# A three-product compression and VectorE sample projections in a one-core NSA / mLSTM step

## The chip, the cores and the metric

The kernel is one launch on one core of a Trainium2 chip. The metric is device time in microseconds (us). A profiled execution gives, beside its time, the start and duration of every instruction on TensorE (PE, with its weight loads PEld), VectorE (DVE), ScalarE (ACT), GpSimd (POOL) and SyncE (SP, which issues most DMAs).

## The reference, cut to what matters

Two layers run for a prompt of 512 tokens and for 8 samples with one new token each, 520 columns in all; the model width is 1024. Layer 0 is native sparse attention, layer 1 an mLSTM, and each adds its output to x. Two places matter here. In layer 0, rows of k and v are compressed: blocks of 32 rows that start every 16 rows, for 1024 cached rows per sample and for the prompt's 512.

```python
seg = rows.reshape(B, n_seg, CMP_STRIDE, 2, N_KV_HEADS, HEAD_DIM)   # segments of 16 rows
w1r = w1f.reshape(2, CMP_R, CMP_STRIDE, HEAD_DIM, CMP_HID)          # CMP_R = 2
part = jnp.einsum('bnrchd,cjrde->bnjche', seg, w1r)
for j in range(CMP_R):
    hid = hid + part[:, j:j + n_cmp, j]
summ = jnp.einsum('bnche,ced->bnchd', jax.nn.silu(hid), w2)
```

So, with A and B the two halves of w1, block i is A s(i) + B s(i+1) over the segments s, then a SiLU and a small second product. In layer 1, q, k and v come from block-diagonal weights, 4x4 blocks over 2048 inner columns:

```python
q = jnp.einsum('btnj,nji->btni', cb, w_qkv[0])   # cb: c = silu(conv) in blocks of 4
k = jnp.einsum('btnj,nji->btni', cb, w_qkv[1])
v = jnp.einsum('btnj,nji->btni', xb, w_qkv[2])   # xb: xm in blocks of 4
```

All results are fp32. The kernel gets that precision from PE either with plain fp32 operands or by splitting each operand into a high and a low part in the fp32r format and summing three fp32r products (`mm3`, L601: hi x hi, hi x lo, lo x hi).

## The kernel before, in words

The program has seven stages, and in each the order of instructions was laid down ahead of time. In four of them a recorder `Rec` (L426) notes every engine call as a piece, where successive PE calls into one PSUM bank form one piece, and then emits the pieces in the order of a written list of numbers (L465). In the other three a `Plan` (L324) holds coarser operations with named dependences, and a list orders those (L352). Each engine works through its own instructions strictly in the order of emission. A second list per stage (MOVED...) names pieces that run on another engine than the code says (`swapped`, L481): an ACT copy goes to DVE, a DVE copy to ACT, and subtractions, multiplications and additions change between DVE and POOL. Counted in order of execution the lists are: 0 CALLS0 (L1028: norm, k/v projections, compression, gates), 1 CALLS2 (L1419), 2 ORDER0 (L1629: attention), 3 CALLS1 (L1956: output projection of layer 0, then the mLSTM's input projection, convolution, SiLU, values, gates), 4 ORDER1 (L2312: z projections, first eight steps over the samples' state matrices), 5 ORDER2 (L2709: the mLSTM cell, the other 24 state steps, most of the output projection) and 6 CALLS3 (L2760: the rest, final norm).

List 0. `kv_tile(i)` (L866) projects one of twelve 128-column tiles of k and v: two chunks of 260 tokens, 24 fp32r products each, scaled out of PSUM into `kvt` on DVE. `cmp_unit(b, c)` (L786) compresses one sample b for k (c = 0) or v (c = 1). It loads eight pages (`praw`), splits them in pieces of 1024 columns into `phi` (ACT) and `plo` (DVE or POOL), and multiplies by w1: 8 row pairs r (two rows of 64 channels fill the 128 partitions), j = 0 and 1 for A and B, and three fp32r products each, N = 256 (4 heads x 64 segments). For j = 1 the same columns are read one to the right, which is why two ones are filled in behind each split. Two of the 16 units carry the prompt's 128 segments too (`xp`), so N = 384. `hidden` (L769) adds the bias and applies the SiLU, and `cmp_second` (L850) makes the second product in plain fp32, 256 columns a unit. `load_w1` (L746) loads and splits one half of w1 and accumulates a constant (`acc`) on DVE in 8 steps. At the start, x arrives in two chunks, is scaled and split (`hhi` on ACT, `hlo` on DVE), and its squares are summed.

List 3. For each of 16 tiles of 128 inner columns `xm_proj` computes xm, `xm_tile` the convolution, `xm_silu` the tile `CT`, `xm_val` (L1826) the values of the prompt with a 128x128 block-diagonal matrix (`block_diag`, L1762, a multiplication on POOL or, moved, on DVE). `xm_gate` (L1837) makes the samples' q, k, v: three plain fp32 products with block-diagonal matrices, 8 columns each, and two copies into `QKS` and `VS`; on every second tile it also adds to the gate sums. Three block diagonals are built per tile (L1910). QKS and VS are read in lists 4 and 5 by `head_open` (L1974), for heads 0 to 3, which are tiles 0-3, 4-7, 8-11 and 12-15.

Of the kernel before, what the change touches and what calls it, by code (L numbers as in the profile page):

```python
# [2869 lines left out]
```

## Time and profile before

| what | value |
|---|---|
| median of 3 timed runs | 1036.99 us (1036.32 to 1039.83) |
| the profiled execution | 1041.29 us, its span 1039.6 us |
| granted TensorE clock | 0.995 |
| DMA, mean | 190 GB/s |
| ACT, POOL busy | 53%, 31% of the span |

All engine work is issued through one helper, so nearly every row bears its line, L507; rows are told apart by the names of the tiles they write and read (`s<-phi,w1h`: PSUM tile s from phi and w1's high part), by shape and count. A plain fp32 product appears with more than one record. "Busy" of a group is the time in which at least one of its instructions runs, "mean" the mean duration of one; the pipeline makes PE's durations longer than the distance between their starts.

### The profile page before, as it was taken

The numbers are of one execution on the slowest core, as the hardware profiler recorded it, in microseconds if no ns is written. First come the engines' busy times: TensorE is split into PE (matmuls) and PEld (weight loads), VectorE is DVE, ScalarE is ACT, GpSimd is POOL, SyncE is SP. The second block draws the span as 40 slices with busy tenths as digits, with TensorE's granted clock in tenths as the row PEclk, the third lists the DMA queues.
The fourth block names the chain that finished last, engine by engine and source line by source line (L and its number), as shares of the span: only waits on it lengthen the run. The fifth ranks groups of instructions, "written<-read, shape, count | busy, mean of one in ns | idle before, by whom it ended". The sixth has DMA issues, their size and how long they took to land.

```text
span 1039.6 us, 23563 instructions
## 1 busy us (share of the span) xinstructions
PE 1016.4 (98%) x8743; PEld 909.5 (87%) x8743; DVE 790.0 (76%) x1903; ACT 553.2 (53%) x1260; POOL 321.7 (31%) x374
## 2 busy tenths in 40 slices
PE   7999999999999999999999999999899999999998
PEld 6999999999998878789999998899766678877897
DVE  7856756586579988964878786775698989888985
ACT  5454344622388788632445444766455564634543
POOL 1233423331232434423331332232332234242330
PEclk9999999999999999999999999999899999999999
DMA  7654644144526344655645253788778698988543
GB/s 256 194 176 156 194 123 130 47 125 135 164 68 198 100 127 130 182 179 184 179 148 171 92 184 121 244 277 289 272 267 276 237 346 287 326 288 276 203 123 113
DMA packets 124789, 197.16 MB, mean 190 GB/s; under 512 B 16117, under 2 KB 66166, under 8 KB 124418
## 3 DMA queue, kind: packets, MB, share of 16 engines
q1 hardware_dynamic: 118866, 186.37, 55.1%
q10 hardware_dynamic: 5808, 9.28, 2.5%
q8 instruction: 69, 1.13, 0.5%
q14 instruction: 46, 0.38, 0.1%
HBM read 145.89 MB, written 58.10 MB: 196 GB/s over the span
## 4 chain that ended last, share of the span: by engine, by line
PE 79%; DVE 10%; ACT 4%; DMA 4%; issue 2%; POOL 1%; SPq 0%; DVEq 0%; ACTq 0%; POOLq 0%
PE mm L507 48%; PE s L507 17%; PE t L507 8%; PE d L507 5%; DVE cs L507 2%; ACT zsg L507 1%; DMA wc<-in_w_qkv 1%; DMA x1d<-x 1%; DVE wlo L507 1%; DVE s L507 1%; DVE hx L507 1%; DMA wraw<-in_m_in 1%; DMA praw<-in_cache 1%; ACT s L507 1%; DVE num L507 0%
## 5 line engine op out<-in xcount | busy, mean ns | idle before, releaser
L507 PE MATMUL mm<-hhi,whi 128*128 128x260 f32 (+1 forms) x952 | 273.5, 287 | 0.9 <-ACT VT L507 0.9
L507 PE MATMUL mm<-hhi,wlo 128*128 128x260 f32 (+1 forms) x952 | 270.6, 284 | 0.1
L507 PE MATMUL mm<-hlo,whi 128*128 128x260 f32 (+1 forms) x952 | 270.1, 284 | 0.0
L507 PEld LDWEIGHTS mm<-hhi,whi 128*128 128x128 f32 (+1 forms) x952 | 179.1, 188 | 5.2 <-issue 2.7
L507 PEld LDWEIGHTS mm<-hhi,wlo 128*128 128x128 f32 (+1 forms) x952 | 179.0, 188 | 0.4 <-DVE wlo L507 0.3
L507 PEld LDWEIGHTS mm<-hlo,whi 128*128 128x128 f32 (+1 forms) x952 | 178.5, 187 | 0.7
L507 POOL TENSOR_TENSOR wlo<-wraw,whi 128x1024 fp32r<-128x1024 f32 (+1 forms) x40 | 78.6, 1967 | 122.1 <-ACT whi L507 39.8
L507 ACT ACTIVATE whi<-wraw 128x1024 fp32r<-128x1024 f32 (+1 forms) x65 | 57.0, 881 | 77.0 <-PE mm L507 33.0
L507 DVE SCALAR_TENSOR_TENSOR cs<-t,wk,cs 128x512 f32<-128x512 f32 x128 | 88.7, 740 | 8.9 <-ACT cs L507 8.3
L507 ACT ACTIVATE cs<-cs,SBC 128x1024 f32<-128x1024 f32 x64 | 71.5, 1142 | 26.8 <-PE d L507 19.6
L507 DVE TENSOR_TENSOR wlo<-wraw,whi 128x1024 fp32r<-128x1024 f32 (+2 forms) x62 | 68.8, 1110 | 11.1 <-ACT whi L507 5.8
L507 PE MATMUL s<-phi,w1h 128*128 128x256 f32 (+1 forms) x256 | 75.8, 296 | 0.0
L507 PE MATMUL s<-plo,w1h 128*128 128x256 f32 (+1 forms) x256 | 74.5, 291 | 1.0 <-DVE plo L507 0.9
L507 ACT ACTIVATE s<-s,mn 128x128 f32<-128x128 f32 (+3 forms) x128 | 70.5, 555 | 6.8 <-DVE mn L507 4.8
L507 PE MATMUL s<-phi,w1l 128*128 128x256 f32 (+1 forms) x256 | 74.0, 289 | 0.0
L507 PE MATMUL mm<-uh,whi 128*128 128x260 f32 x224 | 64.5, 288 | 0.6 <-DVE x L507 0.4
L507 PE MATMUL mm<-uh,wlo 128*128 128x260 f32 x224 | 63.6, 284 | 1.1 <-DVE wlo L507 1.1
L507 DVE CUSTOM_DVE_ANT_0 s<-s,D 128x128 f32<-128x128 f32 (+3 forms) x128 | 58.5, 485 | 7.5 <-PE s L507 5.9
L507 PE MATMUL mm<-ul,whi 128*128 128x260 f32 x224 | 63.4, 283 | 0.0
L507 POOL TENSOR_SCALAR s<-s,sm 128x256 f32<-128x256 f32 (+3 forms) x47 | 42.2, 909 | 52.3 <-DVE sm L507 27.6
L507 PEld LDWEIGHTS s<-plo,w1h 128*128 128x128 f32 x256 | 48.4, 189 | 2.2 <-DVE plo L507 1.5
L507 POOL TENSOR_TENSOR plo<-praw,phi 128x1024 fp32r<-128x1024 f32 (+1 forms) x17 | 30.2, 1775 | 63.6 <-DMA praw<-in_cache 29.8
(485 smaller groups left out, 2632.2 us busy)
## 6 DMA issues: line engine op xcount, KB each, us to landing
cs<-in_state_C SPq DMA_DIRECT2D x64, 512.0 KB, 5.5
o_cs<-cs SPq DMA_DIRECT2D x64, 512.0 KB, 5.6
praw<-in_cache SPq DMA_DIRECT2D x128, 128.0 KB, 2.7
dk<-in_cache SPq DMA_DIRECT2D x128, 128.0 KB, 2.7
wraw<-in_m_in SPq DMA_DIRECT2D x32, 512.0 KB, 3.6
wraw<-in_m_out SPq DMA_DIRECT2D x32, 256.0 KB, 5.2
wraw<-in_w_kv SPq DMA_DIRECT2D x11, 512.0 KB, 4.9
wraw<-in_w_q SPq DMA_DIRECT2D x8, 512.0 KB, 3.6
```

What stands on the lines that cost most here:

```text
L507: return f(*[real(x) for x in a], **{n: real(x) for n, x in k.items()})
```

## The change

With segments paired into even ones e(m) = s(2m) and odd ones o(m) = s(2m+1), the blocks are A e(m) + B o(m) and A o(m) + B e(m+1). The new `cmp_unit(u, c)` takes two samples at once and forms P0 = A o and P1 = B e, each with three fp32r products, and P2 = (A + B)(e + o) in plain fp32, N = 256 each (64 segments of a kind x 4 heads, or 320 with the prompt). Then the even blocks are P2 - P0 - P1 and the odd ones P0(m) + P1(m+1), which costs a copy on ACT and three steps on DVE per unit. The sums e + o (`psm`) and A + B (`w1s`) are made on DVE or POOL. The fills with ones are gone. Eight units of 16 pages (2 buffers) replace sixteen of 8 pages (3 buffers); the second product has 512 columns a unit. Tiles share memory: w1 of the first branch lies in the slot that KA takes later, x in that of KB, A + B in those of VN and VC; `dynamic_dma_scratch_size` is set to 1024. The page layout is rearranged on the host for even and odd segments.

In list 3 the samples' q, k, v leave PE. `xm_gate` copies the 8 sample columns of c and xm into `XS`; `sample_qkv(g)`, called after tiles 7 and 15, shuffles these within groups of four partitions and multiplies and adds per row of the 4x4 blocks on DVE. Only the values' block diagonal is still built.

Of the lists, CALLS0 with MOVED0 and CALLS1 with MOVED1 are new, as their pieces are. ORDER1 and ORDER2 with MOVEDP1 and MOVEDP2 are exchanged for other orders of the same 348 and 933 operations. CALLS2, ORDER0 and CALLS3 hold the same numbers as before.

```diff
-    def load_w1(c, j):
...
+    def load_w1(c):
+        if c:
+            w1a.append(cp.tile([128, 2, 2, 8, 128], F32R, name="w1a", tag="w1a"))
...
+        for j in range(2):
+            raw = wp.tile([128, 8, 128], F32, name="wraw", tag="w", bufs=WRAW + 4)
+            raws.append(raw)
+            SP.dma_start(raw, ap["w1"][:, c, j])
+            pair(w1a[c][:, j, 0], w1a[c][:, j, 1], raw, E[LO_W1[2 * c + j]])
...
+        V.tensor_add(w1s[c], raws[0], raws[1])
```

```diff
+    def cmp_unit(u, c, xp=None):
+        raw = cw.tile([128, 16, 256], F32, name="praw", tag="praw", bufs=2)
+        for k in range(2):
+            pages(0, 2 * u + k, lambda pg, k=k: raw[:, 8 * k + pg], c * 256, 256)
+        W = 64 if xp is None else 80
...
+        def piece(r0, nr, first, last):
...
+            if nr == 2:
...
+                S.activation(hv, rv, AF.Copy)
+                lo_of(lv, rv, hv, e)
             else:
+                for par in range(2):
+                    S.activation(view(hi[:, par]), src(par), AF.Copy)
+                    lo_of(view(lo[:, par]), src(par), view(hi[:, par]), e)
+            (V if r0 % 4 else G).tensor_add(view(sm), src(0), src(1))
...
+            for k in range(nr):
...
+                for m, (out, w, par) in enumerate(((p0, wa, 1), (p1, wb, 0))):
+                    st = a and (m == 0 or xp is not None)
+                    h, l_ = hi[:, par, q], lo[:, par, q]
+                    PE.matmul(out, w[0][:, r0 + k], h, start=st, stop=False, skip_group_check=True)
+                    PE.matmul(out, w[0][:, r0 + k], l_, start=False, stop=False, skip_group_check=True)
+                    PE.matmul(out, w[1][:, r0 + k], h, start=False, stop=z, skip_group_check=True)
+            for k in range(nr):
+                q = slice(N * k, N * k + N)
+                PE.matmul(p2, ws[:, r0 + k], sm[:, q], start=first and k == 0, stop=last and k == nr - 1)
+            R.cut()
+        nr = 2 if xp is None else 1
+        for r0 in range(0, 8, nr):
+            piece(r0, nr, r0 == 0, r0 + nr == 8)
+            if r0 == 2:
+                cmp_second()
...
+        S.activation(t1, p1, AF.Copy)
+        V.tensor_add(t2, p0, t1)
+        V.tensor_add(yv[:, :, 0:W - 1, 1], p0.rearrange("p (h w) -> p h w", h=4)[:, :, 0:W - 1],
+                     t1.rearrange("p (h w) -> p h w", h=4)[:, :, 1:W])
+        V.tensor_sub(yv[:, :, :, 0], p2.rearrange("p (h w) -> p h w", h=4), t2.rearrange("p (h w) -> p h w", h=4))
```

The units and tiles are now recorded as kv 0, unit (0,0), kv 1, unit (1,0) with the prompt, kv 2, unit (2,0), kv 3, unit (3,0), the second branch's w1, KB's clearing, then kv 4 to 11 with units (0,1) to (3,1) and the gates between.

```diff
     def xm_gate(ft):
         ct, xm = CT[ft], xms[ft][1]
-        pq = db()
-        for t, src in enumerate((ct, ct, xm)):
-            PE.matmul(pq[:, 8 * t:8 * t + 8], xst[ft][t], src[:, 512:520], start=True, stop=True)
-        V.tensor_copy(QKS[:, :, ft], pq[:, 0:16].rearrange("p (t b) -> p t b", t=2))
-        V.tensor_copy(VS[:, ft], pq[:, 16:24])
+        V.tensor_copy(XS[:, 0, ft], ct[:, 512:520])
+        V.tensor_copy(XS[:, 1, ft], xm[:, 512:520])
...
+    def sample_qkv(g):
+        f = slice(8 * g, 8 * g + 8)
+        xh = [m1.tile([128, 2, 8, 8], F32, name="xsh", tag="xsh", bufs=4) for j in range(4)]
...
+        for j in range(4):
+            V.stream_shuffle(xh[j].rearrange("p t f b -> p (t f b)"), XS[:, :, f],
+                             [4 * (p // 4) + j for p in range(32)])
+        for j in range(4):
+            wq = wqt[:, 0:2, f, j].unsqueeze(3).to_broadcast([128, 2, 8, 8])
+            wv = wqt[:, 2, f, j].unsqueeze(2).to_broadcast([128, 8, 8])
+            xq = xh[j][:, 0:1].to_broadcast([128, 2, 8, 8])
+            V.tensor_mul(tq if j else QKS[:, :, f], wq, xq)
+            V.tensor_mul(tv if j else VS[:, f], wv, xh[j][:, 1])
+            if j:
+                V.tensor_add(QKS[:, :, f], QKS[:, :, f], tq)
+                V.tensor_add(VS[:, f], VS[:, f], tv)
...
-        xst[ft] = [block_diag(mi, wc0[:, t, ft], "bd", 12) for t in range(3)]
+        xst[ft] = block_diag(mi, wc0[:, 2, ft], "bd", 4)
```

More of the change, by code (lines that the diff above doesn't have):

```diff
@@ L709, in step_kernel @@
     cw = pool_of(cctx, name="cmpw", bufs=2)
-    xc, wkv = [], {}
+    wkv = {}
     raw0 = wp.tile([128, 8, 128], F32, name="wraw", tag="w", bufs=WRAW + 4)
-    for c in range(2):
-        xc.append(cw.tile([128, 2080], F32, name="x_t", tag="praw", bufs=3).rearrange("p (k t) -> p k t", k=8))
     for k in range(2):
@@ L767, in load_w1 @@
         V.tensor_scalar(hncst[:, c:c + 1], hcst[:, c:c + 1], -1.0, None, op0=OP.mult)
-    def hidden(out, psrc, c, shape):
-        s = cw.tile(shape, F32, name="hsg", tag="hsg")
-        sigmoid_into(s, psrc, sbias=hncst[:, c:c + 1])
-        V.scalar_tensor_tensor(out, psrc, hcst[:, c:c + 1], s, op0=OP.add, op1=OP.mult)
     def pages(row, u, dst, col, n):
@@ L822, in part @@
-        def part(k, j, start, stop):
-            hi, lo = parts[k]
-            for r in range(nr):
-                q = slice(nc_ * r + j, nc_ * r + j + nc_)
-                mm3(po[:, 0:nc_], w1[c][j][0][:, nr * k + r], w1[c][j][1][:, nr * k + r], hi[:, q], lo[:, q],
-                    start and r == 0, stop and r == nr - 1)
-        if xp is not None:
-            order = [(k, j) for k in range(4) for j in range(2)]
-        else:
-            order = ((0, 0), (1, 0), (0, 1), (1, 1)) if b == 0 else ((0, 0), (0, 1), (1, 0), (1, 1))
@@ L834, in cmp_unit @@
-        for n, (k, j) in enumerate(order):
-            if k not in parts:
-                split(k)
-            part(k, j, n == 0, n == len(order) - 1)
-            R.cut()
-            if n == 1:
-                cmp_second()
-        hs = cw.tile([128, 4, 64], F32, name="hs", tag="hs")
-        G.memset(hs[:, :, 63:64], 0.0)
-        hidden(hs[:, :, 0:63], pw[:, :, 0:63], c, [128, 4, 63])
-        if xp is not None:
-            hidden(HP[:, c, :, 0:31], po[:, 256:384].rearrange("p (h t) -> p h t", h=4)[:, :, 0:31], c, [128, 4, 31])
@@ L846, in cmp_unit @@
-        second.append((b, c, hs))
+                for par in range(2):
+                    S.activation(view(hi[:, par]), src(par), AF.Copy)
+                    lo_of(view(lo[:, par]), src(par), view(hi[:, par]), e)
+            (V if r0 % 4 else G).tensor_add(view(sm), src(0), src(1))
+            if xp is not None:
+                ev, od = (xp[:, r0, par].rearrange("p (h m) -> p h m", h=4) for par in range(2))
+                for par, x in ((0, ev), (1, od)):
+                    hv, lv = (t[:, par].rearrange("p (h w) -> p h w", w=W)[:, :, 64:80] for t in (hi, lo))
+                    S.activation(hv, x, AF.Copy)
+                    lo_of(lv, x, hv)
+                V.tensor_add(sm.rearrange("p (h w) -> p h w", w=W)[:, :, 64:80], ev, od)
@@ L848, in step_kernel @@
+        s = cw.tile([128, 4, 2 * W - 1], F32, name="hsg", tag="hsg", bufs=1)
+        sigmoid_into(s, y, sbias=hncst[:, c:c + 1])
+        V.scalar_tensor_tensor(y, y, hcst[:, c:c + 1], s, op0=OP.add, op1=OP.mult)
+        G.memset(Y[:, :, 63:128:64], 0.0)
+        if xp is not None:
+            V.tensor_copy(HP[:, c, :, 0:31], Y[:, :, 128:159])
+        second.append((u, c, Y))
     second = []
@@ L983, in step_kernel, with kv @@
             PE.matmul(pss[:, :CH], ones, acc, start=True, stop=True)
-        rms_factor(pss, cw, rr[c], tag="hsg", bufs=2, cold=True)
+        rms_factor(pss, cw, rr[c], tag="hp1", bufs=1, cold=True)
     R.at("w1", 0)
-    load_w1(0, 0)
-    load_w1(0, 1)
-    R.at("cmp", 0, 0)
-    cmp_unit(0, 0)
-    R.at("cmp", 1, 0)
-    cmp_unit(1, 0)
-    b = 2
-    for i in range(12):
+    load_w1(0)
+    cell = {}
+    def kv(i):
         br, hp = divmod(i, 2)
@@ L1006, in step_kernel, with unit @@
             v_nat(t, hp, 0 if br == 3 else 1)
[L1007 to L1017 removed]
+    def unit(u, c, xp=None):
+        R.at("cmp", u, c)
+        cmp_unit(u, c, xp)
+    kv(0)
+    unit(0, 0)
+    kv(1)
+    unit(1, 0, XP[0])
+    kv(2)
+    unit(2, 0)
+    kv(3)
+    unit(3, 0)
+    R.at("w1", 1)
+    load_w1(1)
+    KA = kvp.tile([128, 4, 1024], F32R, name="KA", tag="KA")
+    KB = kvp.tile([128, 4, 1024], F32R, name="KB", tag="KB")
+    G.memset(KB.bitcast(F32), 0.0)
+    VN = kvp.tile([128, 2, 4, 4, 64], F32, name="VN", tag="VN")
+    kv(4)
+    unit(0, 1)
+    kv(5)
+    kv(6)
+    unit(1, 1, XP[1])
+    kv(7)
+    kv(8)
+    unit(2, 1)
+    kv(9)
+    kv(10)
     R.at("gates")
     gates()
[L1020 to L1023 removed]
+    unit(3, 1)
+    kv(11)
     R.at("second")
@@ L1026, in step_kernel @@
     R.at("out")
+    VC = kvp.tile([128, 4, 4, 64], F32, name="VC", tag="VC")
+    G.memset(VC, 0.0)
+    VCS = kvp.tile([128, 4, 2, 128], F32, name="VCS")
     cmp_out()
```

166 lines of the change are left out of this document (72 added, 94 removed), and 311 rows, old and new, of tables (CALLS0, CALLS1, CALLS3, MOVED0).

## The prediction

> **What bounds the kernel now.** I read the page first, then the busy time by stage, the chain of waits inside two stages, and the groups by form of the stages that the change touches.
>
> ```profile
> span 1039.6 us, 23563 instructions
> PE 1016.4 (98%) x8743; PEld 909.5 (87%) x8743; DVE 790.0 (76%) x1903; ACT 553.2 (53%) x1260; POOL 321.7 (31%) x374
> ```
>
> A busy PE on this page counts pipelined ends, so 98% only says that PE seldom stands empty. The stages say more (columns: length, then busy time and instruction count of PE, weight load, DVE, ACT and POOL):
>
> ```profile
> 0.00:12.00 12.00, 6.16 (x14) 3.85 (x14) 4.78 (x12) 6.34 (x14) 3.84 (x6) 1.00 0.86 287
> 12.00:27.00 15.00, 15.00 (x122) 14.84 (x121) 14.69 (x28) 9.77 (x21) 0.00 (x0) 1.00 0.72 230
> 27.00:202.00 175.00, 173.42 (x1360) 169.34 (x1358) 114.86 (x228) 81.19 (x194) 56.02 (x52) 1.00 0.47 146
> 507.00:643.00 136.00, 135.07 (x1185) 131.37 (x1187) 104.70 (x234) 67.87 (x149) 42.93 (x57) 0.99 0.45 145
> 747.00:998.00 251.00, 247.42 (x1748) 188.97 (x1749) 221.26 (x482) 130.02 (x218) 76.06 (x83) 0.99 0.81 273
> ```
>
> I cut the stretches where the lists meet: list 0 (compression and the k/v projections) ends at 202 us, list 3 at 643, list 4 at 747, list 5 at 998. In 27 to 202 DVE is 66% busy and ACT 46%; in 12 to 27 DVE is as full as PE. The chain of waits inside the stages of lists 0 and 3, and then of list 5:
>
> ```profile
> by line: PE s L507 50.4%; PE mm L507 29.7%; PE t L507 5.0%; DMA praw<-in_cache 3.0%; DMA wraw<-in_w_kv 2.6%; DVE plo L507 1.6%; POOL wlo L507 1.4%; ACT hsg L507 1.1%; ACT phi L507 1.1%; DVE acc L507 0.7%; ACT VT L507 0.6%; issue 0.5%; POOL
> ```
> ```profile
> by line: PE mm L507 52.7%; PE t L507 12.4%; PE d L507 6.6%; DMA x1d<-x 6.0%; PE s L507 5.2%; DMA wraw<-in_m_in 3.8%; DVE cva L507 2.7%; ACT whi L507 2.2%; SPq L507 2.0%; DVE wlo L507 1.7%; issue 1.0%; ACT cvs L507 0.8%; ACT cva L507 0.7%; D
> ```
> ```profile
> by line: PE mm L507 44.4%; PE s L507 9.1%; PE t L507 7.9%; DVE cs L507 7.3%; PE d L507 5.5%; issue 4.4%; DVE hx L507 2.3%; DVE num L507 2.0%; DMA wraw<-in_m_out 1.4%; DVE wlo L507 1.3%; ACT cs L507 1.3%; DVE kwl L507 1.2%; DVE dn L507 1.2%;
> ```
>
> In list 0 85% of the chain is PE, half of the stretch the compression's own products ("s"). In list 3 it is 77%, and 6.6% of it is "d", the samples' q, k, v products that the change deletes. List 5 has 67% PE, with DVE's state rows (cs) next. So PE work taken out of lists 0 and 3 should shorten them until DVE or a transfer is late; for list 5, which computes what it did, only the order counts.
>
> **Compression, PE.** Prices come from starts of successive instructions, since a single one's duration includes the pipeline's ends. Chain and timeline rows, then groups:
>
> ```profile
> 27.49 5.72 PE s L507 x48
> ```
> ```profile
> 63.40 0.34 PE L507 MATMUL s<-phi,w1h 128*128 128x384 f32 x1
> ...
> 64.11 0.34 PE L507 MATMUL s<-plo,w1h 128*128 128x384 f32 x1
> ```
> ```profile
> 945.40 2.16 PE s L507 x8
> ```
> ```profile
> L507 PE MATMUL s<-q,CT 128*128 128x512 f32 x32 | 16.6, 599 | 0.0
> ```
> ```profile
> L507 PE MATMUL s<-phi,w1h 128*128 128x256 f32 x224 | 64.6, 288 | 0.0
> L507 PE MATMUL s<-phi,w1h 128*128 128x384 f32 x32 | 11.1, 348 | 0.0
> ```
>
> A 256-column fp32r product takes 5.72/48 = 0.119 us, and a 384-column one (64.11 - 63.40)/4 = 0.178. Plain fp32: the code issues 16 products q x CT of 512 columns and the trace holds 32, so each goes through in two passes; the eight records at 945.40 are two passes over 512+384+256+128 columns, 2.16/2560 = 0.84 ns a column and pass, so 256 columns cost 0.43 us, against 3 x 0.119 = 0.36 for the three-part fp32r product.
>
> Before: 3 x 224 x 0.119 + 3 x 32 x 0.178 = 80.0 + 17.1 = 97.1 us. After: each of 8 units (two samples, one branch) has 8 row pairs with two fp32r triples and one fp32 product, 2 x 0.36 + 0.43 = 1.15; six units of 256 columns give 55.2. Two units carry the prompt, 320 columns: a triple is 3 x 0.148 (midway), the fp32 one 0.54, together 1.43, so 22.9. Sum 78.1: **PE -19.0 us**. The second product is half as often and twice as wide, nothing either way.
>
> **Compression, the other engines.** These rows are the stage's DVE and POOL groups:
>
> ```profile
> L507 DVE TENSOR_TENSOR plo<-praw,phi 128x1024 fp32r<-128x1024 f32 x18 | 26.0, 1452 | 14.6 <-ACT phi L507 12.1 <-DMA praw<-in_cache 1.3 <-ACT xp L507 1.0
> L507 DVE TENSOR_TENSOR plo<-praw,phi 128x256 fp32r<-128x256 f32 x9 | 4.3, 477 | 0.9 <-ACT phi L507 0.9
> L507 DVE SCALAR_TENSOR_TENSOR acc<-wraw,pe,acc 128x128 f32<-128x128 f32 x30 | 12.6, 421 | 1.1 <-DMA wraw<-in_w 0.8
> L507 DVE TENSOR_TENSOR kvt<-mm,rr 128x260 f32<-128x260 f32 x21 | 8.7, 420 | 5.2 <-PE mm L507 4.3 <-DMA o_kv<-kvt 0.6 <-DVE KB L507 0.2
> L507 DVE CAST phi<-ones 128x2 fp32r<-128x2 f32 x18 | 7.6, 421 | 3.6 <-PE s L507 3.6
> L507 DVE CAST plo<-ones 128x2 fp32r<-128x2 f32 x16 | 4.6, 290 | 1.7 <-PE s L507 0.9 <-issue 0.8
> L507 DVE CAST phi<-praw 128x1024 fp32r<-128x1024 f32 x7 | 7.5, 1076 | 5.7 <-issue 3.4 <-PE s L507 1.2 <-DMA praw<-in_cache 0.7
> L507 DVE SCALAR_TENSOR_TENSOR hlo<-x_t,nw,hhi 128x260 fp32r<-128x260 f32 x16 | 6.9, 483 | 0.2 <-ACT hhi L507 0.2
> L507 DVE TENSOR_TENSOR w1l<-wraw,w1h 128x1024 fp32r<-128x1024 f32 x3 | 3.6, 1216 | 0.0
> L507 DVE TENSOR_TENSOR sq<-sq 128x260 f32<-128x260 f32 x7 | 3.0, 425 | 0.9 <-POOL sq L507 0.8
> L507 DVE COPY VN<-t 128x512 f32<-128x512 f32 x1 | 0.7, 682 | 0.0
> ```
> ```profile
> L507 POOL TENSOR_TENSOR plo<-praw,phi 128x1024 fp32r<-128x1024 f32 x10 | 24.4, 2441 | 41.5 <-DMA praw<-in_cache 16.6 <-PE s L507 14.1 <-ACT phi L507 10.8
> ```
>
> Gone are 34 fills with ones on DVE, 7.6 + 4.6 = 12.2 us. I counted new list 0 out against the order in which the program records its pieces. It leaves on DVE: 20 sums e+o of 512 columns at 0.68 (as VN) = 13.6; 13 of 256 at 0.42 and 10 small ones at about 0.2 = 7.5; 27 steps that take P0, P1, P2 apart, at the price of kvt 0.42 = 11.3; 13 more 256-column low halves at 0.48 = 6.2; two more 1024-column ones = 2.9; one weight sum 1.2. Against that stand three fewer 1024-column casts at 1.08 and small change from casts, hidden steps and copies that are fewer or moved, by the same rows about -8 in all. Net +22: DVE now does 4.78 + 14.69 + 114.86 = 134 us, then 156, of a stage of about 193. That is 81%, where 747 to 998 runs at 221.26/251 = 88%. So DVE should not bind on average, and I charge +2 us of waits (0 to 8). The first k tile's split into KA now waits for the first branch's w1, whose slot it takes; only the next stages read KA, so this is covered, as is KB's clearing on POOL, moved to the middle of the stage.
>
> **Start of list 0.** Now PE is fed from 12 to 27 with k/v tiles 0, 1 and part of 2 (122 records) and meets the first compression product at 27.5. The new list puts only k/v tile 0 (48 products, 5.8 us) ahead of it, and that first product needs all 16 pages of two samples, both halves of w1, and on DVE, ahead of its low half: 16 hlo x 0.483, 13 squares and adds x 0.425, w1's two low halves and sum 3 x 1.216, 7 acc x 0.421, two half-width weight lows 2 x 0.68, then its own 1.22: 7.7 + 5.5 + 3.6 + 2.9 + 1.4 + 1.2 = 22 us. DVE has 19.5 us done at 27 now, so it would reach this at 27 to 30. PE then has 120 x 0.12 - 5.8 = 8.6 us less done than now. It can't be caught up, because later PE has no slack to fill: **+8 us** (3 if DVE starts 5 us sooner, 11 if it ends at 30). List 0 in all: -19 + 8 + 2 = **-9**.
>
> **Samples' q, k, v.** PE loses three fp32 8-column products and DVE or ACT two copies per tile:
>
> ```profile
> 638.19 0.59 PE L507 MATMUL d<-CT,bd 128*128 128x8 f32 x4
> 638.64 0.37 PE L507 MATMUL d<-xm,bd 128*128 128x8 f32 x2
> 638.93 0.41 PE L507 MATMUL s<-CT,FG 128*32 128x260 f32 x1
> 640.39 0.61 PE L507 MATMUL d<-CT,bd 128*128 128x8 f32 x4
> 641.08 0.60 PE L507 MATMUL t<-sr,cst 128*128 128x24 f32 x4
> ```
> ```profile
> L507 DVE TENSOR_TENSOR bd<-cst,wc x28: 274/283/1843, 531.8 to 638.4; 128x128 f32<-128x128 f32 x28
> L507 POOL TENSOR_TENSOR bd<-cst,wc x20: 394/405/846, 523.7 to 634.2; 128x128 f32<-128x128 f32 x20
> ```
> ```profile
> L507 DVE COPY QKS<-d x5: 157/165/174, 598.1 to 642.9; 128x16 f32<-128x16 f32 x5
> L507 DVE TENSOR_TENSOR pr<-QKS x4: 176/178/181, 647.0 to 895.4; 128x32 f32<-128x32 f32 x4
> ```
>
> Starts give 0.74 and 0.69 us per tile, 16 of them 11.4; the chain has 6.6% of 143 = 9.4. On DVE and POOL 32 block diagonals of 48 go. The new list leaves 12 on POOL and 4 on DVE, so DVE saves 24 x 0.283 = 6.8 and POOL 8 x 0.405. Added: 32 copies of 8 columns (as QKS<-d, 0.165) in place of 32 copies out of PSUM: nothing. 8 shuffles and 28 multiplies and adds of 64 or 128 columns, the latter at bd's 0.283: 36 x 0.25 = 9. The trace has no shuffle; between the 0.165 of a copy and four times 0.283 the eight cost 1.3 to 9, and I take 0.283, the same-size row. The new list gives part of these to POOL, so DVE's 104.7 of 136 stays near that, of a stage 9 us shorter. They stand behind convolution work in DVE's queue, but their readers, the state steps of heads 0 and 1 (first group) and 2 and 3 (second), come in lists 4 and 5, so nobody waits. One more 98 KB load on SP is hidden behind 145 GB/s. **-8** (-11 to -2): 9.4 less 1.4 for weight low halves that are now due sooner.
>
> **Lists 4 and 5.** The computation is the same, the orders differ, and so do the operations that change engine. In list 5 DVE ends with some 16 fewer 512-column operations:
>
> ```profile
> L507 DVE TENSOR_TENSOR wlo<-wraw,whi 128x512 fp32r<-128x512 f32 x12 | 8.2, 681 | 0.4 <-ACT rs_y L507 0.4
> ```
> ```profile
> L507 POOL TENSOR_TENSOR wlo<-wraw,whi 128x512 fp32r<-128x512 f32 x13 | 17.3, 1327 | 36.4 <-PE mm L507 16.0 <-ACT whi L507 11.8 <-DVE whi L507 5.3
> ```
>
> 16 x 0.681 = 11 us leave the engine that is second on the chain, and 16 x 1.327 = 21 land on POOL (76 of 251 busy), each 0.65 later for whoever waits. I take 0, from -7 to +7: those 11 us less 4, or as much lost.
>
> **Sum.** -9 - 8 + 0 = -17. The profiled execution took 1041.3 us (span 1039.6), 4.3 above the median of the timed runs, 1037.0. Profiled 1024.3, median **1020.0**. The terms' ends spread by 8, 4 and 7; together about 11, so this case alone spans 1009 to 1031.
>
> **Rivals.** *DVE and POOL block each other in list 0.* A 1024-column subtract takes 1.216 where nothing reads beside it (w1l) and 1.452 on average as plo; the 2-column fills show 0.421 and 0.290. Both engines' work on SBUF, put end to end: DVE 156, less what reads PSUM (24 kvt and 27 steps x 0.42, copies 6) = 129, plus POOL's 56 less the six 1024-column low halves x 2.44 that leave it = 41, is 170. From 7 us on (12 - 4.8) that ends at 177, below 193, so without gaps it doesn't bind. At the 88% of list 5 it ends at 200, and list 0 gains 2 instead of 9. With DVE's PSUM work queued behind it as well (156 + 41, 204) list 0 gains nothing: 1037 - 8 = 1029, which I take. The Trainium skill, "SBUF — State Buffer", section "Who interferes with whom", says that a DVE instruction with two SBUF inputs and a GpSimd instruction that reads SBUF exclude each other for a whole instruction. By that rule the new DVE sums, each with two SBUF inputs, speak against the change and the time is this rival's 1029; the trace agrees as far as 1.216 against 1.452 goes. 16%, 1022 to 1036.
>
> *The start costs nothing.* If pages and w1 come early and DVE's small operations slip between, the 8 us go: 1012. Against it: DVE was full from 12 to 27. 14%.
>
> *Slower: list 5's chain.* New list 5 moves 255 of 265 DVE operations, by 9 places in the mean; a place is 221.26/482 = 0.46 us, so an operation on the chain that slid back by the mean hands over 4.1 us late. Four such use up the 17; five make 1037 + 3.6 = 1040.6, and six 1044.7. For it: DVE's cs, hx and num are 11.6% of that chain. Against: moves go both ways and DVE has less to do. 10%.
>
> *The change doesn't do what it says:* were fp32 to need four passes, 64 products x 0.43 more is +28: 1048. Two records per product speak against it. 4%.
>
> **Chances.** Forecast 56%, blocking 16%, free start 14%, slower 10%, four passes 4%. Run to run this kernel moves by about 0.3% (1036.32 to 1039.83), so "same" is 1033.9 to 1040.1: 3 of the blocking case's points and 4 of list 5's fall there, 0.07. Slower: 6 + 4 = 0.10. Faster: 0.83. For 8 in 10 I take the forecast's range, widened to 1006 for the free start with good lists and to 1035 for the blocking case.
>
> **What would show it.** Right: the 768 fp32r records of the compression become 384, with 128 fp32 ones beside them, list 0 ends near 193, list 3 takes about 8 less, no "d<-CT,bd" is left, the rest keeps its lengths. The start is right if the first phi product comes near 28 with PE empty ahead of it, and DVE has some 156 us in list 0. Wrong: DVE's idle time small and PE's waits in list 0 put down to plo or the sums; list 5 longer by several us with DVE releasing PE; or a shuffle of over 1 us.

## The result and the profile after

The changed kernel takes 1009.83 us (median of 4 runs, 1009.16 to 1011.65), the kernel before 1037.63 in the same rounds: a ratio of 0.9736, 95% interval 0.9716 to 0.9757, or 27.4 us less (25.2 to 29.5). The forecast was 17 us less. The page of the changed kernel begins:

```profile
span 1007.4 us, 22794 instructions
PE 983.7 (98%) x8375; PEld 871.3 (86%) x8375; DVE 800.9 (80%) x1946; ACT 546.8 (54%) x1219; POOL 342.6 (34%) x412
```

PE lost 32.7 us of busy time and 368 records, DVE gained 11 us, and PE is still 98% busy: what PE lost is what the span lost. The busy time by stage of the changed kernel shows where (columns as before: length, then PE, weight load, DVE, ACT and POOL, then granted clock, DMA share, GB/s):

```profile
0.00:12.00 12.00, 6.33 (x18) 4.51 (x18) 6.15 (x17) 7.14 (x15) 0.66 (x6) 1.00 0.86 279
12.00:27.00 15.00, 10.32 (x53) 8.88 (x53) 13.55 (x29) 9.08 (x18) 0.00 (x0) 0.89 0.71 223
27.00:189.00 162.00, 160.56 (x1150) 149.04 (x1150) 136.27 (x284) 80.77 (x156) 57.39 (x59) 1.00 0.50 158
493.50:617.50 124.00, 123.50 (x1091) 119.11 (x1089) 103.33 (x233) 63.52 (x149) 43.47 (x60) 1.00 0.49 159
721.50:966.00 244.50, 242.30 (x1746) 187.76 (x1747) 209.42 (x459) 130.50 (x220) 91.62 (x103) 1.00 0.83 281
```

List 0 ends at 189 us (202 before), the part of list 3 that held the samples' products takes 124 (136), list 5 takes 244.5 (251). DVE has 6.15 + 13.55 + 136.27 = 156 us in list 0, to the microsecond what was forecast. In 12 to 27 us PE has 53 records where it had 122. The groups by form of list 0, changed kernel:

```profile
L508 PE MATMUL s<-phi,w1a 128*128 128x256 f32 x192 | 39.4, 292 | 0.5 <-DVE w1a L508 0.4
L508 PE MATMUL t<-psm,w1s 128*128 128x256 f32 x96 | 23.0, 379 | 0.0
L508 DVE TENSOR_TENSOR plo<-praw,phi 128x1024 fp32r<-128x1024 f32 x20 | 25.1, 1264 | 4.6 <-ACT phi L508 4.3
L508 DVE TENSOR_TENSOR psm<-praw 128x512 f32<-128x512 f32 x20 | 13.6, 685 | 0.1
L508 DVE CAST KA<-kvt 64x512 fp32r<-64x512 f32 x8 | 11.3, 1417 | 0.1
L508 POOL TENSOR_TENSOR plo<-praw,phi 128x1024 fp32r<-128x1024 f32 x4 | 10.6, 2657 | 13.5 <-PE s L508 5.1 <-ACT hp L508 4.6 <-DMA praw<-in_cache 3.7
```

The sums e + o (`psm`) cost 0.685 us each, as the copy of the same width did. The 96 records of `t<-psm,w1s` are two for each of 48 fp32 products, 0.216 us apart by their starts, the 0.84 ns a column of the forecast. So a plain product costs 0.43 us, and the rival that doubles this price is out; what a record is inside PE, the trace does not show. The groups of list 3, changed kernel, hold the new shuffle and its neighbours; the shuffle takes 0.294 us, where 0.283 was assumed:

```profile
L508 DVE STREAM_SHUFFLE xsh<-XS 128x128 f32<-128x128 f32 x8 | 2.4, 294 | 0.0
L508 DVE TENSOR_TENSOR xtq<-wqt,xsh 128x128 f32<-128x128 f32 x4 | 1.2, 288 | 0.1
```

For a finer account I gave each PE record the time until the next record starts, so that a wait is charged to the record ahead of it, and summed by kind. In list 0 the compression's first products went from 101.6 us (768 records) to 80.6 (384 fp32r records, 128 fp32 ones): -21.0. The projections of k, v and the gates, the same 624 products, went from 77.3 to 85.0: +7.7, all of it before 25 us, where 48 of them now take 13.6 us that would take 48 x 0.12 = 5.8 back to back (what fills the rest is read under "What sets the start"). Everything else together changed by 0.4. In list 3 the samples' products were 10.8 us and are gone.

**A part of the difference of the two traces is no change at all.** The traces differ by 32.2 us, the timed runs by 27.4. The windows of before show why; the first and the third row are the stretches in which a wait of PE begins (the second wait lasts until 747.0), the others those right behind:

```profile
573.00:589.00 16.00, 15.14 (x129) 15.05 (x128) 11.71 (x20) 6.42 (x17) 8.94 (x8) 1.00 0.43 137
589.00:593.00 4.00, 4.00 (x24) 4.00 (x23) 2.90 (x9) 2.03 (x4) 0.00 (x0) 0.57 0.09 34
741.00:745.00 4.00, 3.10 (x62) 2.80 (x60) 1.67 (x6) 2.09 (x5) 0.94 (x2) 1.00 0.80 271
745.00:753.00 8.00, 5.99 (x18) 2.93 (x19) 5.14 (x30) 2.18 (x8) 1.28 (x4) 0.58 0.72 262
```

The granted clock falls to 0.57 for 4 us and to 0.58 for 8 us: 4 x 0.43 + 8 x 0.42 = 5.1 us, where PE has work all the time. That is no full account of the 4.3 us by which the profiled execution of before lay above its median: the timed runs of before have granted clocks of 0.995 to 1.0, 2.5 to 3.2 us below the full clock in the mean of each round, so half clock is 2 to 3 us of the 4.3. PE's waits ahead of them in before were these:

```profile
PE mm L507 <- ACT VT L507: 0.9, 1, 0.9
```
```profile
PE t L507 <- DVE pr L507: 2.9, 1, 2.9
```

The changed kernel's profile has reduced clock in the first 27 us only (0.89 in 12 to 27). So stages are compared below with undisturbed ones.

### The profile page after: what moved, and what is told of

Same layout as the page of the kernel before. It is cut to its first block, busy times and chain, and to the rows that moved or that the text cites. A ratio compares the mean times of both kernels' runs of the same rounds, so it can differ in the third digit from the quotient of the medians.

```text
span 1007.4 us, 22794 instructions
## 1 busy us (share of the span) xinstructions
PE 983.7 (98%) x8375; PEld 871.3 (86%) x8375; DVE 800.9 (80%) x1946; ACT 546.8 (54%) x1219; POOL 342.6 (34%) x412
## 4 chain that ended last, share of the span: by engine, by line
PE 85%; DVE 6%; DMA 3%; issue 2%; ACT 2%; POOL 1%; SPq 1%; DVEq 0%; POOLq 0%; ACTq 0%
PE mm L508 55%; PE s L508 13%; PE t L508 11%; PE d L508 6%; DMA x_t<-in_xT 1%; DVE num L508 1%; DMA praw<-in_cache 1%; DVE s L508 1%; DVE plo L508 1%; SPq L508 1%; DMA wraw<-in_m_in 0%; DMA wraw<-in_w_kv 0%; DVE wlo L508 0%; DVE ul L508 0%; DVE x L508 0%
## 5 line engine op out<-in xcount | busy, mean ns | idle before, releaser
L508 POOL TENSOR_TENSOR wlo<-wraw,whi 128x512 fp32r<-128x512 f32 (+1 forms) x41 | 76.4, 1866 | 117.9 <-DVE whi L508 52.1
L508 DVE SCALAR_TENSOR_TENSOR cs<-t,wk,cs 128x512 f32<-128x512 f32 x128 | 89.1, 743 | 13.1 <-ACT cs L508 11.4
L508 ACT ACTIVATE whi<-wraw 128x1024 fp32r<-128x1024 f32 (+1 forms) x58 | 51.0, 883 | 53.4 <-PE mm L508 16.0
L508 PE MATMUL s<-phi,w1a 128*128 128x256 f32 (+1 forms) x224 | 50.6, 301 | 1.5 <-ACT phi L508 1.0
L508 PE MATMUL mm<-uo,whi 128*128 128x260 f32 x256 | 46.4, 284 | 0.0
L508 DVE TENSOR_TENSOR x<-x,mm 128x260 f32<-128x260 f32 x72 | 28.6, 418 | 22.4 <-PE mm L508 18.2
L508 PEld LDWEIGHTS mm<-uh,whi 128*128 128x128 f32 x224 | 42.2, 188 | 2.5 <-DVE num L508 0.8
L508 PEld LDWEIGHTS mm<-uh,wlo 128*128 128x128 f32 x224 | 42.1, 188 | 1.7 <-DVE wlo L508 1.7
```

The costliest lines, as they stand in the source:

```text
L508: return f(*[real(x) for x in a], **{n: real(x) for n, x in k.items()})
```

## Experiments

The table gives, from each trace, the end of list 0 (its last PE record), and the lengths of list 3 (first product of the output projection to the last transposition ahead of the state steps), list 4 (to the first product `mm<-CT,bdm`) and list 5 (to the first `s<-uh,whi`); then the median time, and its ratio to before in the same rounds with the 95% interval. Lists 1, 2 and 6 take 99.2 to 99.9, 158.2 to 158.6 and 40.6 to 40.8 us in all of them; list 1 takes 99.2 behind the old list 0 and 99.9 behind the new one. A star marks a length that holds a stretch of reduced clock worth 0.5 us or more, in list 0 behind its first 27 us (ahead of that, every kernel with the new list 0 has one).

| kernel | list 0 | list 3 | list 4 | list 5 | median us | ratio to before |
|---|---|---|---|---|---|---|
| before | 201.9 | 182.5* | 106.3* | 250.6* | 1037.63 | 1 |
| changed | 189.0 | 170.2 | 104.7 | 244.5 | 1009.83 | 0.9736 (0.9716-0.9757) |
| compression alone | 189.6 | 180.5* | 105.4 | 247.9 | 1023.92 | 0.9883 (0.9864-0.9902) |
| samples alone | 201.7 | 170.6 | 105.0* | 247.5* | 1022.37 | 0.9863 (0.9848-0.9879) |
| lists 4, 5 alone | 201.0 | 180.2 | 105.9* | 246.9* | 1031.38 | 0.9953 (0.9937-0.9970) |
| changed, old lists 4, 5 | 188.9 | 170.3 | 104.6 | 247.1 | 1012.48 | 0.9755 (0.9738-0.9771) |
| changed, old list 4 | 189.3 | 170.1 | 104.7 | 246.1* | 1010.72 | 0.9749 (0.9727-0.9771) |
| changed, no sample work | 188.9 | 170.0 | 104.3 | 243.9 | 1009.57 | 0.9749 (0.9725-0.9774) |
| changed, P2 in fp32r | 191.2* | 172.2 | 105.4 | 245.7 | 1014.58 | 0.9781 (0.9764-0.9799) |
| the same, no low halves | 176.6* | 171.0 | 105.4 | 246.8* | 999.24 | 0.9617 (0.9597-0.9637) |
| changed, branch 0 in fp32 | 194.6 | 170.2 | 104.9 | 244.7* | 1014.87 | 0.9775 (0.9755-0.9795) |
| both of these edits | 190.8* | 170.2 | 104.8 | 244.0 | 1011.52 | 0.9766 (0.9743-0.9789) |
| P2 fp32r, both branches fp32 | 181.6 | 170.4 | 104.7 | 244.0 | 1003.12 | 0.9685 (0.9662-0.9708) |
| changed, pages in two loads | 189.8 | 170.3 | 104.7 | 245.3* | 1010.77 | 0.9738 (0.9722-0.9754) |

### The three parts taken apart

The compression's new code with CALLS0 and MOVED0; the samples' new code with CALLS1 and MOVED1; ORDER1, ORDER2, MOVEDP1 and MOVEDP2: each alone in the kernel before. The first two carry the scratch size of 1024 as well, so its share is in both and was not run by itself.

```diff
 compression alone:  + cmp_unit(u, c), load_w1(c), slots, page layout; CALLS0, MOVED0
 samples alone:      + XS, sample_qkv(g), w_qkvT;                      CALLS1, MOVED1
 lists alone:        + ORDER1, MOVEDP1, ORDER2, MOVEDP2
```

> The kernel before with the compression by three half products alone (new list 0). Theory A: list 0 ends at 189 instead of 202, as in the full change, because PE has 17 us less to do there and only 4 us more idle, nearly all of it before 27 us; the time falls by 13 us. Theory B (the forecast on record): 9 us, with 8 lost at the start and 2 in waits. If the three parts are independent, the gains of this run, of the samples alone and of the lists alone sum to the 27.8 us of the full change; if they are not, the sum differs by more than 4 us.

> The kernel before with the samples' q, k, v on VectorE alone (new list 3). Theory A: list 3 loses the 48 small products of 9.4 to 11.4 us and nothing is late for it, so list 3 goes from 184 us to about 172 and the time falls by 10 to 12 us. Theory B (the forecast on record: 1.4 us and more are given back where weight low halves are due sooner): -8. Theory C (part of the 13.5 us seen in list 3 of the full change belongs to an earlier stage, which leaves transfers or weights in a better state): -6 or less. The 8 shuffles take about 0.29 us each.

> The kernel before with the new lists 4 and 5 alone (ORDER1, ORDER2 and the operations that change engine in them); all else as before. In the traces list 5 went from 251 to 244.5 us, list 4 stayed at 104. Theory A (the new order and the 16 or so operations that leave DVE make list 5 shorter, whatever comes ahead of it): list 5 takes about 245 us here too, and the time is 4 to 7 us below before. Theory B (the lists bring nothing: the profiled execution of before was 4.3 us over its median, with a granted clock of 0.99 in lists 3 and 5, and that is the difference): list 5 takes 245 to 249 us in both, and the time is within 3 us of before. The forecast on record put this term at 0, from -7 to +7. Lists 0 to 3 are unchanged and should end at 202, 300, 459 and about 642 us.

Measured against before: compression -12.1 us (-10.2 to -14.1), samples -14.2 (-12.5 to -15.8), lists -4.9 (-3.1 to -6.5). In the traces each part changes its own stage: compression alone ends list 0 at 189.6 us, as the full change does; samples alone brings list 3 to 170.6, as the full change does. Theory A holds for the compression. For the samples it holds for the stage, but the time falls by more than its 10 to 12 us; the part of theory C that puts their gain in an earlier stage is out. The lists alone are inside the 4 to 7 us of their theory A, with the 3 us of theory B at the edge of the interval. The undisturbed old list 3 is that of the lists alone, 180.2, so the samples' work in the list itself is worth -10.0 (the other two old ones, less 1.7 us of half clock each, are 180.8 and 178.8, so this holds to about 1 us). The timed gain is 2.5 to 5.8 us more. One piece of that is seen: in all profiles with the old list 3 PE waits once for a value copy, 1.0 us beyond its usual step, and in two of the three (before, and compression alone at 573 to 580 us, clock 0.76) the half clock follows, worth 1.7 us; in the profiles with the new list it does not come in this list. The granted clocks of the timed runs agree with a piece of that size: they are 1.2 us below the full clock in the mean with the samples alone and 2.5 in before. The rest, 1 to 4 us, stays open.

The three gains alone sum to 31.2 us against 27.4: they are independent to within 4 us, which is what their intervals can tell.

### Lists 4 and 5

Two kernels from the other side: the changed one with both old lists, and with the old list 4 only.

```diff
 changed, old lists 4, 5:  ORDER1, MOVEDP1, ORDER2, MOVEDP2 of before
 changed, old list 4:      ORDER1, MOVEDP1 of before
```

> The changed kernel with the lists 4 and 5 of before. If the lists' gain is their own (the run of the lists alone gave 4.9 us, between 3 and 6.5), this run is 3 to 6.5 us slower than the changed kernel, 1013 to 1016, and lists 4 and 5 take about 353 us together instead of 349. If the three parts overlap (their gains alone, 12.1, 14.2 and 4.9, sum to 31 instead of 27.5), this run is within 2 us of the changed kernel: what the lists gain alone, a shorter wait for pr at the end of list 4 and the granted clock after it, one of the other parts has removed already.

> The changed kernel with list 4 alone of before (its order and its operations that change engine); list 5 stays new. In the traces so far list 5 takes 244 to 245.7 us with the new list and 247 to 248 with the old one, where PE's clock is whole, and PE's wait for pr at the end of list 4 is 2.19 us with the new lists and 3.12 with the old. Theory A (the two gains are separate): list 5 stays at 244 to 246, the wait for pr is 3.1 us again, the time is about 1 us above the changed kernel. Theory B (list 5 is shorter because the new list 4 hands over to it in a better state): list 5 takes 247 us or more, and the time is 2 to 4 us above the changed kernel.

The old lists cost 0.9755 - 0.9736, or 2 us, with both intervals some 2 us wide to either side; so the time alone leaves open whether these lists gain 5 us or none, and it falls between the two expectations (3 to 6.5 us, or under 2). The traces are sharper. Windows of list 5 in the changed kernel with the old lists:

```profile
721.90:969.00 247.10, 244.40 (x1746) 188.30 (x1745) 221.22 (x482) 130.01 (x218) 76.22 (x82) 1.00 0.83 277
```

With the new list, above, it is 244.5 us long; DVE does 12 us less there and POOL 15 more, and PE's busy time falls by 2.1. Where the clock is whole, list 5 takes 247.1 and 247.9 with the old list (two kernels) and 243.9 to 245.7 with the new one (five), and between the two kernels that differ in lists 4 and 5 alone it is 2.6 us. With the old list 4 only it takes 246.1; the window behind its beginning in that kernel is

```profile
722.20:726.00 3.80, 3.80 (x8) 1.53 (x6) 3.12 (x18) 1.61 (x5) 0.00 (x0) 0.63 0.98 286
```

A clock of 0.63 costs 3.8 x 0.37 = 1.4 us there; without it list 5 would take 244.7, as with the new list 4. So the gain seen in the traces is list 5's own, theory A. PE's waits at the end of list 4, first with both old lists, then in the changed kernel:

```profile
PE t L510 <- DVE pr L510: 2.9, 1, 2.9
```
```profile
PE t L508 <- DVE pr L508: 2.1, 1, 2.1
```

The new list 4 shortens this wait by 0.9 us (0.8 in these rows) in every profile, yet list 4 takes 104.6 to 105.4 us with the old list and 104.3 to 105.4 with the new one, where the clock is whole: no difference shows. This wait too is followed by half clock in some executions and not in others.

### Does anybody wait for the samples' q, k, v?

```diff
-            V.stream_shuffle(xh[j]...)            # and the 28 multiplies and adds
+            V.memset(QKS[:, :, f], 1.0); V.memset(VS[:, f], 1.0)
```

> The changed kernel without the work that makes the samples' q, k, v: the 8 shuffles and 28 multiplies and adds are left out (q, k and v of the samples are set to one by 4 small fills), the 32 copies stay. DVE and POOL lose about 10 us in list 3. Theory A (nobody waits for that work; the forecast has it at nothing): the time is within 2 us of the changed kernel and list 3 stays at 170 us. Theory B (DVE's 103 us of 124 in the later part of list 3 hold PE up): list 3 is 2 us or more shorter.

List 3 stays at 170.0 us (170.2), and the time is the changed kernel's to within 2 us, by the medians and by the ratios: nobody waits for this work. Theory A.

### What sets list 0 now: PE alone?

Five kernels take work from PE, from DVE, or from both, all from the changed one. P2's sums are written as fp32r, so that one pass at the fp32r rate multiplies them; then, on top, the low halves of pages and prompt are left out:

```diff
-    w1s = [kvp.tile([128, 8, 128], F32, name="w1s", tag=k) ...]
+    w1s = [kvp.tile([128, 8, 128], F32R, name="w1s", tag=k) ...]
-            sm = cw.tile([128, n], F32, name="psm", ...)
+            sm = cw.tile([128, n], F32R, name="psm", ...)
 no low halves:
-                lo_of(lv, rv, hv, e)
-                    PE.matmul(out, w[0][:, r0 + k], l_, ...)
+                    PE.matmul(out, w[0][:, r0 + k], h, ...)
```

> The changed kernel with the third product, (A+B)(e+o), as one fp32r product of rounded sums instead of one plain fp32 product: it leaves out the low parts of both sums, and nothing else changes, in DVE's and POOL's work neither. PE loses about 48 x (0.43 - 0.117) + 16 x (0.54 - 0.147) = 21 us in list 0. Theory A (PE sets list 0, 177 of its 189 us busy, and DVE with 156 has room): list 0 ends 15 to 21 us sooner. Theory B (DVE and POOL, in each other's way on their shared side, are close behind PE: 129 us of DVE's work on SBUF plus 41 of POOL's from 7 us on end at 177): list 0 ends at 177 or later, at most 12 us sooner, and PE's idle time grows by the rest. Theory C (DVE is the bound already): no gain.

> The kernel of the third product in fp32r, and in it no low halves of pages and prompt either: it leaves these 62 subtracts of list 0 out (27 + 11 + 5 = 43 us of DVE), and PE multiplies the high half a second time in their place, so PE's work is that of the third product in fp32r, 21 us below the changed kernel. There list 0 still ended at 191. Theory A (what stood in PE's place there is DVE: 157 us of work in 191, with the low halves late for PE): without the 43 us list 0 ends 15 us or more sooner, at 176 or earlier, and PE's gaps in the stage after 27 us fall from 24 us to under 10. Theory B (it is the order laid down in the list, or the arrival of pages and weights): list 0 ends at 185 or later.

With 21 us less for PE list 0 ended 2 us later, not 21 or 12 sooner. PE's waits after 27 us in this kernel (the changed one has 1.4 us of them in all), the longest of nine:

```profile
PE s L508 <- DVE plo L508: 6.0, 3, 5.3
PE mm L508 <- DVE wlo L508: 2.2, 3, 1.6
PE mm L508 <- DVE hs L508: 1.7, 1, 1.7
PE t L508 <- DVE psm L508: 1.7, 3, 0.6
```

and the windows from 27 to 120 us:

```profile
27.00:60.00 33.00, 28.96 (x191) 26.21 (x190) 31.04 (x92) 20.91 (x50) 5.67 (x9) 0.95 0.63 201
60.00:90.00 30.00, 27.70 (x223) 26.62 (x221) 25.23 (x38) 18.13 (x24) 10.39 (x5) 1.00 0.65 210
90.00:120.00 30.00, 24.19 (x164) 22.91 (x165) 23.95 (x51) 8.97 (x18) 10.49 (x16) 0.89 0.60 194
```

Where PE ran ahead it met DVE: 31 of 33 us busy at the beginning, as in the changed kernel (31.95), and the low halves (`plo`) late. The longest wait is one of 5.3 us:

```profile
91.22 2.38 POOL L508 TENSOR_TENSOR wlo<-wraw,whi 128x1024 fp32r<-128x1024 f32 x1
91.33 3.36 DVE L508 TENSOR_TENSOR plo<-praw,phi 128x1024 fp32r<-128x1024 f32 x1
94.74 0.58 PE L508 MATMUL s<-plo,w1a 128*128 128x256 f32 x1 [5.27 <-DVE plo L508]
```

DVE was busy nearly all that time (13.95 of 15 us from 80 to 95), and the low half that PE wanted took 3.36 us instead of 1.22 beside a POOL subtraction. Then the clock falls (0.95, 0.89), which takes part of what PE had saved. Without the low halves, 43 us of DVE's work and 24 of POOL's, list 0 ends at 176.6, 14.6 sooner, with the window

```profile
27.00:176.60 149.60, 141.58 (x1078) 135.02 (x1077) 100.40 (x221) 79.77 (x156) 30.85 (x33) 0.98 0.54 171
```

So the low halves stood in PE's place, most of them on DVE; how much is DVE's own work and how much its meeting with POOL is not taken apart. All these kernels keep the changed kernel's order of instructions; whether an order laid for the cheaper P2 would do better was not run. Theory C of the first expectation holds for this order, and A of the second, which just misses its mark: 176.6 us for 176, and 12 us of gaps by PE's starts where under 10 was said. Next, less for DVE at a price for PE: the first branch's P0 and P1 in plain fp32 straight from the raw pages, alone and together with P2 in fp32r; and both branches so.

```diff
-                    h, l_ = hi[:, par, q], lo[:, par, q]        # three fp32r products
+                    pr = raw[:, :, o:o + 16].rearrange("p g (x s) -> p x g s", s=4)
+                    PE.matmul(out, wr[1 - par][:, r0 + k], pr, ...)   # one plain fp32 product
```

> The changed kernel, with the first branch's (c = 0) half products all in plain fp32 from the raw weights and the raw pages: no high and low halves of w1 and of the pages there. It computes the same. PE: 96 products of 256 columns at 0.43 instead of 3 x 0.117 and 32 of 320 at 0.54 instead of 3 x 0.147, about +5.5 to 8 us; DVE and POOL lose about 17 us of low halves of 1024 columns, 10 of smaller ones and 2.4 of w1's; ACT about 25. Theory A (list 0 of the changed kernel waits for DVE's work, in its first half above all, and for the chain w1, high half, low half before the first product): the start is 1 to 3 us sooner, the gaps after 27 us shrink, and the time is within 4 us of the changed kernel either way, since PE has 177 + 6 of 189. Theory B (PE alone sets list 0): 5 to 8 us slower than the changed kernel.

> Both edits on the changed kernel that did nothing or harm alone: the third product in fp32r of rounded sums (PE -21 us in list 0; it leaves out the low parts of the two sums, so this product is less precise) and the first branch's half products in plain fp32 from raw weights and pages (DVE -26 us, PE +5.5). Alone they made list 0 191 and 195 us against 189. Theory A (PE with 177 us and DVE with its low halves at PE's heels each set list 0, so that only less of both helps): list 0 ends at 165 to 178 and the time falls below the changed kernel by 11 to 22 us, to 988 to 999. Theory B (the effects simply add, or the order and the arrival of data set it): list 0 ends at 190 or later.

> As the run with the third product in fp32r and the first branch's half products in plain fp32, but with both branches' half products in plain fp32 (the third product again leaves out the low parts of the sums). PE: 177 - 21 + 11 = 167 us, DVE about 105 us. Theory A (with DVE out of the way PE alone sets list 0: its work and the 11 us lost before 27 us): list 0 ends at 175 to 181, and this is 2 to 6 us slower than the run with one branch, if that was bound by PE already, or up to 5 faster, if DVE still bound it in its second half. Theory B (order and arrival): as that run.

Alone it costs the 5.6 us in list 0 that PE's work grows by (5.5 to 8 were worked out), although DVE has 24 us less, with this window:

```profile
27.00:194.50 167.50, 165.09 (x1111) 151.18 (x1110) 112.84 (x235) 63.86 (x116) 51.99 (x54) 1.00 0.48 152
```

In time it is 4 us slower by the ratios, 5 by the medians, so theory B is nearer. In the changed kernel PE sets list 0: its busy time there grows by 6.0 us (177.2 to 183.3) and the list by 5.6, so DVE's 24 us less bring half a microsecond at most. And DVE is so close behind that, in this order, less for PE gains nothing either. Both edits together were to break that, and the expected 165 to 178 did not come: 190.8, theory B's mark (190 or later). PE's longest wait there, and DVE's part of the timeline ahead of its end at 95.7 us:

```profile
PE s L508 <- DVE plo L508: 6.8, 2, 6.5
```
```profile
87.36 0.69 DVE L508 CAST phi<-praw 128x1024 fp32r<-128x1024 f32 x1 [6.01 <-DMA praw<-in_cache]
87.97 1.29 DVE L508 TENSOR_TENSOR psm<-praw 128x512 fp32r<-128x512 f32 x2
...
91.47 2.38 POOL L508 TENSOR_TENSOR wlo<-wraw,whi 128x1024 fp32r<-128x1024 f32 x1
91.58 2.82 DVE L508 TENSOR_TENSOR psm<-praw 128x512 fp32r<-128x512 f32 x1
...
94.58 1.21 DVE L508 TENSOR_TENSOR plo<-praw,phi 128x1024 fp32r<-128x1024 f32 x1
```

At the change to the second branch DVE stood idle for 6 us until its pages came, then worked through its list, one 512-column sum stretched from 0.69 to 2.82 us beside a POOL subtraction, before the low half that PE wanted. Much of the first branch's gain was lost there, to the pages' arrival and to the order, as theory B has it. With both branches unsplit that chain is gone:

```profile
27.00:181.60 154.60, 150.60 (x1013) 138.58 (x1012) 88.35 (x189) 50.62 (x92) 27.98 (x32) 1.00 0.51 165
```

List 0 ends at 181.6 us, just past theory A's 175 to 181, and the time is 8 us below the run with one branch, where at most 5 were expected; DVE is busy for 107 us of it, PE for 168.7. The kernel takes 1003.12 us, a ratio of 0.9685 (0.9662 to 0.9708): below both kernels, 0.5% below the changed one. It pays with a third product of rounded sums.

### What sets the start

```diff
             def one(i=i):
+                if u < 2 and row == 0 and col == 0 and whole is not None:
+                    if i == 0:
+                        SP.dma_start(whole, ap["cache"][8 * u:8 * u + 8, :, 0:n]...)
+                    return
```

> The changed kernel, with the 16 pages of the first two samples' first branch loaded by two transfers of eight neighbouring pages each; it leaves out 16 look-ups in the page table (these pages are then the cache's first sixteen), so SP issues 2 transfers where it issued 16 between 5 and 26 us. Theory A (the first compression product, at 25.2 us, waits for pages that SP issues one by one and for the second half of w1 that stands behind eleven of them): the first product comes at 21 us or earlier and the time falls by 2 to 5 us. Theory B (DVE sets the start, as the forecast on record has it, or the bytes that must land before it, 4.7 MB at about 350 GB/s): the first product comes at 24 us or later and the time stays within 2 us of the changed kernel.

The start of list 0 in the changed kernel, from its timeline:

```profile
18.02 2.10 PE L508 MATMUL s<-sq,ones 128*128 128x260 f32 x4 [3.42 <-ACT sq L508]
```
```profile
16.74 0.43 SPq L508 DMA_DIRECT2D wraw<-in_w  x1
17.35 5.21 SPq L508 DMA_DIRECT2D praw<-in_cache  x8
...
22.23 1.06 ACT L508 ACTIVATE w1a<-wraw 128x1024 fp32r<-128x1024 f32 x1 [2.52 <-DMA wraw<-in_w]
22.23 1.23 DVE L508 TENSOR_TENSOR w1s<-wraw 128x1024 f32<-128x1024 f32 x1 [1.37 <-DMA wraw<-in_w]
...
24.10 2.01 ACT L508 ACTIVATE phi<-praw 128x1024 fp32r<-128x1024 f32 x2 [0.81 <-DMA praw<-in_cache]
...
25.22 0.39 PE L508 MATMUL s<-phi,w1a 128*128 128x256 f32 x1
...
26.48 0.38 PE L508 MATMUL s<-plo,w1a 128*128 128x256 f32 x1 [0.87 <-DVE plo L508]
```

ACT and DVE both wait for the second half of w1, which SP issues at 16.74 us behind eleven pages and which lands at 22.2. ACT then waits for pages that land at 24.1, and has the first high half at 25.1; DVE makes the low half from 25.2 on, for which PE waits 0.9 us more. But PE is no sooner: its 48 projections end at 24.9. Of the 7.7 us that they lose, 3.6 go in a wait for the squares of x's second chunk (the first row), and 1.5 in 16 products that come every 0.216 us, as at half clock, instead of every 0.12. So three chains, PE's own, the pages' and w1's, end within 0.3 us of each other. With two loads in place of sixteen the window from 12 to 27 us is

```profile
12.00:27.00 15.00, 8.96 (x45) 7.93 (x45) 13.45 (x29) 8.91 (x19) 0.00 (x0) 0.77 1.03 343
```

at 343 GB/s instead of 223: the transfers are full, the second chunk of x comes later (PE waits 11.5 us in all for the squares of x, 9.1 in the changed kernel), and the first product comes at 27.4 us, not 21. It follows the last projection without a wait, although the high half had been ready since 23.7 us:

```profile
27.24 0.28 PE L508 MATMUL mm<-hhi,wlo 128*128 128x260 f32 x1
27.36 0.28 PE L508 MATMUL s<-phi,w1a 128*128 128x256 f32 x1
```

Theory A falls. Theory B's marks are met, but by PE's own chain: x's second chunk, issued at 9.0 and 9.1 us in the two kernels, is used from 17.4 us on instead of 14.35, while the DMA moves 357 GB/s with the pages asked for ahead of it. List 0 ends only 0.8 us later, and the time is the changed kernel's.

## Why the prediction was right, and where its sizes were off

The direction, the stages and the range held. The gain was larger by 10 us: the time lies at the low end of the forecast's own 1009 to 1031, as three terms missed on the same side. By the steps of the forecast:

- **PE -19.0 in the compression.** Right: -21.0 with the waits that the records hold. Without waits the forecast has 97.1 and 78.1, so by the forecast's prices these records held some 4.5 us of waits before and 2.5 after.
- **Start +8.** Right in size (+7.7) and in what is lost (48 products ahead of the first compression product, at 25.2 us instead of 27 to 30), wrong in the reason, so that the size is partly luck. I counted 22 us of DVE's operations; DVE has 1.4 us of idle just ahead of the sum of w1, because the second half of w1 has not landed. What PE lost was mostly a wait of 3.6 us for x's second chunk and 1.5 us at a slow clock, which the forecast does not have, and DVE's and the pages' chains happened to end when PE's did. The run with two page loads shows that the pages cannot simply be issued sooner.
- **Waits +2.** This step failed: by the account above 2 us fewer, not 2 more. DVE's 156 us, 83% of the stage, left PE idle for 1.4 us after 27 us (1.6 before). Steps 1 to 3 give -21.0 + 7.7 + 0.4 = -12.9 instead of -9. The rival of DVE and POOL blocking each other did not decide, but its picture was right in part one step further on: in the run with P2 in fp32r 2.1 us of the longest wait are a low half that POOL stretched, the rest DVE's own queue.
- **Samples -8.** The products were 10.8 us, inside the 9.4 to 11.4; of the 1.4 us charged for weights due sooner, 0.8 came (list 3 is 10.0 shorter than the undisturbed old one). That the shuffles and multiplies are free held.
- **Lists 4 and 5, 0.** Mis-sized by about 2.6 us, in list 5, where DVE hands 12 us to POOL and PE's stage gets shorter. The rival in which moved operations cost 4.1 us each did not come.
- **Profile and median.** I subtracted the difference of 4.3 us as a constant. Some 2 to 3 us of it was half clock behind two waits, of which this execution had more than the timed runs. With list 1, which takes 0.7 us more behind the new list 0, -12.9 + 0.7 - 10.0 - 2.6 = -24.8; the timed -27.4 (25.2 to 29.5) leaves some 2.6 us open. Whether half clock that no longer comes is in it is not shown: the changed kernel's four timed runs are 3.5 us below the full clock in the mean, those of before 2.5 to 3.2, and how much of the 3.5 lies in the start of list 0 only the one profile tells (about 1.7).

## What to carry to other kernels

When PE is 98% busy, work taken off PE is worth its length only up to the next engine's pace in the same stage: here 21 us taken off PE's products shortened list 0 by 12.9, as its new start lost 7.7, and the next 21 gained nothing in the same order, since DVE was at 156 of 189 us with low halves due at once. Test the wall by taking work off each engine in turn, then off both. And compare stages, not spans, between single profiles: a short wait of PE can draw a stretch of half clock that makes one profile several microseconds longer than the next.
